# The channel mixer's first product by one level of Strassen's algorithm, its second product as a stage of its own

## The chip, the core and the metric

The kernel runs on one core of one Trainium2 chip. A core has five engines with instruction streams of their own: TensorE (PE, matrix products; PEld is its loading of weights), VectorE (DVE), ScalarE (ACT), GpSimd (POOL) and SyncE (SP), which issues DMA transfers. An engine takes its instructions in order; instructions of different engines wait for one another by semaphores. On-chip memory is SBUF (128 partitions) and PSUM (eight banks of 512 float32 per partition), in which TensorE accumulates. The metric is the device time of one execution in microseconds, by the median of several runs.

## What is computed

The reference is one layer of a hybrid model on 1024 tokens of width 1024, with 16 learned tokens ahead. Three token mixers, their gates and `w_mix_out` come first; the channel mixer `conv_ffn` is the last stage:

```python
def rms_norm(x, g):
    x32 = x.astype(jnp.float32)
    y = x32 * lax.rsqrt(jnp.mean(x32 * x32, axis=-1, keepdims=True) + EPS)
    return (y * g.astype(jnp.float32)).astype(x.dtype)
...
def conv_ffn(x, w_up, dw_w, dw_b, w_down):
    h = causal_dwconv(x @ w_up, dw_w, dw_b)
    a, b = jnp.split(h, 2, axis=-1)
    return (jax.nn.silu(a) * b) @ w_down
...
        h = h + (g1 * y_hg + g2 * y_at + g3 * y_cv) @ w_mix_out[l]
        h = h + conv_ffn(rms_norm(h, norm2_g[l]), w_ffn_up[l], ffn_dw_w[l], ffn_dw_b[l], w_ffn_down[l])
    return h[:, N_META:]
```

`w_ffn_up` is 1024 x 5632 (the halves a and b of 2816 columns each), `w_ffn_down` 2816 x 1024, `w_mix_out` 1024 x 1024. The depthwise convolution has three taps in the direction of the tokens, so the first token needs two of the learned ones ahead of it: the mixer works on 1026 tokens.

## The kernel before

All three products are made to float32 accuracy out of a faster format: every operand is split into a high part and the rest (hi on ScalarE, a rounding copy; lo on VectorE or GpSimd, a subtraction), and `mm3` makes three products for each block of 128 rows of the contraction: hi x hi, hi x lo, lo x hi.

The stages before are phase 1 (norm, projections, two of the token mixers), phase 2 (attention and the sum of the three branches into `y`), the token mix and the channel mixer.

- **Token mix** (`ysplit`, `mix`, `norm2`). `ysplit` makes hi and lo of `y` (tile `yt`) in three chunks of tokens. `mix` runs over four groups of 256 output columns; for each it loads and splits four panels of `w_mix_out` (`panel`: raw tile `wur`, split tile `wu`, the lo on GpSimd) and makes 24 products (8 k x 3) of 256 columns for each of the 8 tiles of 128 tokens, and a small product for the two learned tokens (tile number -1). VectorE adds the result (PSUM tile `one`) to the residual `h1`, ScalarE sums squares. In the fourth group each tile goes straight on to `norm2`: the reciprocal root by some eleven VectorE steps on one column, ScalarE scales two half tiles (`xs`), TensorE transposes them, VectorE multiplies by the norm's gain, ScalarE and GpSimd or VectorE split the result into `x2`.
- **Channel mixer** (`up0`, `up`, `gate`, `down`). Panel pair j (of 22) is 128 columns of a and 128 of b. For each half `up` makes 3 chunks x 8 k x 3 products of 342 columns into PSUM tile `up` (`one` in `up0`, which is used for j = 0 and 1); ScalarE and VectorE apply the taps from PSUM (`ypad`), `gate` applies silu and the product, and splits the hidden panel (`hid`). `down` multiplies pairs of hidden panels by two rows of `w_ffn_down` (tile `wd`): 8 token tiles x 2 column halves x 2 panels x 3 products of 512 columns, into PSUM tile `dn`; VectorE adds each to `h1`. So `down` of two former panels runs among the `up` products of the next two; `down` of the last panel writes the output.

The order of each engine's instructions is set by a list scheduler, which takes what is ready by the program's order and by `high_priority`; tiles share memory by pools, and a pool that is opened where another was closed makes its first writer wait for the last reader of the old one (`reuse_waits`).

## Time and profile before

| | |
|---|---|
| median of 3 runs | 2007.42 us (2006.85 to 2009.17) |
| the profiled execution | 2008.94 us, of which the profile's span is 2007.1 us |
| busy, TensorE / VectorE / ScalarE / GpSimd | 96% / 64% / 37% / 18% |
| token mix, from its first product | at 1142.34 us |
| channel mixer, from the end of the last `w_mix_out` product | from about 1245.56 us to the end |

A profile is one execution. Times are microseconds from the start of the span. A matmul's end is modelled, so that the time between two starts is the better measure of TensorE's pace; in square brackets a row of the timeline names the engine's idle time before it and the instruction that ended it. The granted clock is TensorE's, as a share of full speed: its two levels are 1.2 and 2.4 GHz, so 0.52 over a stretch means that nearly all of it ran at the lower.

### The profile page before, as it was taken

The numbers are of one execution on the slowest core, as the hardware profiler recorded it, in microseconds if no ns is written. First come the engines' busy times: TensorE is split into PE (matmuls) and PEld (weight loads), VectorE is DVE, ScalarE is ACT, GpSimd is POOL, SyncE is SP. The second block draws the span as 40 slices with busy tenths as digits, with TensorE's granted clock in tenths as the row PEclk, the third lists the DMA queues.
The fourth block names the chain that finished last, engine by engine and source line by source line (L and its number), as shares of the span: only waits on it lengthen the run. The fifth ranks groups of instructions, "written<-read, shape, count | busy, mean of one in ns | idle before, by whom it ended". The sixth has DMA issues, their size and how long they took to land.

```text
span 2007.1 us, 31950 instructions
## 1 busy us (share of the span) xinstructions
PE 1925.3 (96%) x12592; PEld 1827.0 (91%) x12592; DVE 1275.3 (64%) x2661; ACT 745.1 (37%) x1559; POOL 360.8 (18%) x380
## 2 busy tenths in 40 slices
PE   5999999999999998899999899999999999999998
PEld 5989999998999998788999799899999999999997
DVE  7577988999887953547666615654554455445545
ACT  4456888212421243535454534521222122212210
POOL 4232122443423311212342222000000000000000
PEclk8999999999999999889999999999999999999999
DMA  4233332221111227453332311210111011111102
GB/s 152 51 93 100 104 101 57 65 64 48 38 46 37 64 82 157 122 140 102 102 96 58 121 43 38 90 48 29 61 54 48 27 59 58 43 31 58 55 5 84
DMA packets 153125, 142.03 MB, mean 71 GB/s; under 512 B 7178, under 2 KB 140765, under 8 KB 152334
## 3 DMA queue, kind: packets, MB, share of 16 engines
q1 hardware_dynamic: 141822, 128.27, 22.3%
q0 software_dynamic: 11152, 11.71, 2.4%
q8 instruction: 99, 1.62, 0.3%
q14 instruction: 52, 0.43, 0.1%
HBM read 108.64 MB, written 31.31 MB: 70 GB/s over the span
## 4 chain that ended last, share of the span: by engine, by line
PE 61%; DVE 9%; DMA 4%; issue 1%; ACT 1%; POOL 1%; SPq 0%; POOLq 0%; ACTq 0%; DVEq 0%
PE up L74 23%; PE dn L74 11%; PE mm L74 9%; PE one L74 7%; DVE A L835 5%; PE gt L74 2%; PE pv L1054 2%; PE pt L1044 2%; PE S L1027 2%; DMA wgr<-in_w_in_dram 1%; DMA cv_d<-H 1%; PE at L62 1%; DVE Q L762 1%; DVE att L747 1%; PE one L89 0%
## 5 line engine op out<-in xcount | busy, mean ns | idle before, releaser
L74 PE MATMUL up<-x,wu 128*128 128x342 f32 x2880 | 477.9, 320 | 0.0
L74 PEld LDWEIGHTS up<-x,wu 128*128 128x128 f32 x2880 | 463.1, 189 | 12.6
L74 PE MATMUL gt<-xn,wg 128*128 128x342 f32 x2016 | 355.1, 326 | 13.6 <-ACT tg L910 6.5
L74 PEld LDWEIGHTS gt<-xn,wg 128*128 128x128 f32 x2016 | 321.3, 190 | 18.9 <-ACT tg L910 8.4
L74 PE MATMUL dn<-wd,hid 128*128 128x512 f32 x1008 | 257.7, 393 | 1.4 <-DVE h L1355 1.3
L1355 DVE TENSOR_TENSOR h<-dn,h 128x512 f32<-128x512 f32 x176 | 120.9, 687 | 191.9 <-PE dn L74 191.7
L74 PEld LDWEIGHTS dn<-wd,hid 128*128 128x128 f32 x1008 | 184.4, 188 | 32.1 <-DVE h L1355 2.9
L835 DVE SCALAR_TENSOR_TENSOR A<-H,cvw,A 128x256 f32<-128x256 f32 (+2 forms) x210 | 186.2, 916 | 1.8
L122 ACT ACTIVATE wu<-wur 128x512 fp32r<-128x512 f32 x104 | 65.0, 627 | 310.3 <-PE up L74 284.3
L1322 DVE SCALAR_TENSOR_TENSOR ypad<-up,fpar,ypad 128x1026 f32<-128x1026 f32 x80 | 102.5, 1281 | 64.8 <-ACT ypad L1320 64.7
L1319 POOL MEMSET ypad<- 128x2 f32 x40 | 4.0, 99 | 648.6 <-DVE ypad L1330 600.5
L123 DVE TENSOR_TENSOR wu<-wur,wu 128x512 fp32r<-128x512 f32 x88 | 60.5, 688 | 89.9 <-ACT wu L122 88.6
L74 PE MATMUL mm<-bT,wo 128*128 128x386 f32 (+2 forms) x576 | 109.1, 333 | 4.9 <-ACT bT L1124 3.4
L74 PE MATMUL mm<-xn,wm 128*128 128x256 f32 (+1 forms) x768 | 101.5, 288 | 3.5 <-DVE g L551 2.0
L513 DVE TENSOR_SCALAR_CACHE_REDUCE jd<-sc,cb 128x912 bf16<-128x912 f32 (+1 forms) x124 | 102.6, 828 | 3.2
L74 PE MATMUL mm<-xn,wc 128*128 128x260 f32 x768 | 101.3, 286 | 2.5 <-DVE Q L636 2.5
L74 PEld LDWEIGHTS mm<-bT,wo 128*128 128x128 f32 x576 | 95.2, 195 | 7.9 <-ACT bT L1124 4.2
L74 PEld LDWEIGHTS mm<-xn,wm 128*128 128x128 f32 x768 | 96.7, 191 | 4.0 <-DVE Q L636 3.9
L74 PEld LDWEIGHTS mm<-xn,wc 128*128 128x128 f32 x768 | 95.4, 189 | 3.1 <-DVE Q L636 2.8
L74 PE MATMUL one<-wu,yt 128*128 128x256 f32 x768 | 94.3, 282 | 1.8 <-ACT yt L1214 1.2
L74 PEld LDWEIGHTS one<-wu,yt 128*128 128x128 f32 x768 | 91.8, 188 | 2.3 <-ACT yt L1214 1.4
L511 ACT ACTIVATE ja<-sc,cb 128x1040 bf16<-128x1040 f32 (+2 forms) x93 | 84.5, 909 | 14.1 <-DVE cb L518 8.0
(383 smaller groups left out, 2994.9 us busy)
## 6 DMA issues: line engine op xcount, KB each, us to landing
...
```

Source lines behind the costliest of these rows:

```text
L62: self.nc.tensor.matmul(*args, **kw)
L74: self.nc.tensor.matmul(ps, x(k), y(k), start=first and i == 0 and j == 0, stop=last and i == n - 1 and j == 2)
L122: nc.scalar.activation(hl[:, 0], raw, AF.Copy)
L123: (lo or nc.vector).tensor_tensor(hl[:, 1], raw, hl[:, 0], op=OP.subtract)
L511: nc.scalar.activation(ja[:, :n], self.sc[j], AF.Sign, scale=-1.0, bias=T0[:, c], accum_out=cnt[:, c])
L513: nc.vector.tensor_scalar(jd[:, :n], self.sc[j], T0[:, c], 0.0, op0=OP.is_lt, op1=OP.add, accum_out=cnt[:, c])
L835: nc.vector.scalar_tensor_tensor(acc, h, self.cvw[:, c, k:k + 1], acc, op0=OP.mult, op1=OP.add)
L1027: nc.tensor.matmul(pS[:, :w], qs[:, h, :], kst[:, part, s], start=part == 0, stop=part == 1)
L1044: nc.tensor.transpose(pt[:kn, a, i, :], P[i][:, k0:k0 + kn], self.ident)
L1054: nc.tensor.matmul(pv[:, 0:256], vt[:kn, kt, :], pT[:kn, part, a].rearrange("p a b -> p (a b)"), start=g == 0 and a == 0 and part == 0, st ...
L1322: nc.vector.scalar_tensor_tensor(v3(o), u3, wt(2 - o), v3(o), op0=OP.mult, op1=OP.add)
L1355: nc.vector.tensor_tensor(self.h1[i][:, ns], pd, self.h1[i][:, ns], op=OP.add)
```

## The change

**The first product.** For one pair j the product is a matrix of 256 rows (128 of a, 128 of b) by 1026 tokens over 1024 of contraction. It is cut in two in the direction of the contraction (4 k each), in rows (a and b), and the tokens are cut into four pieces of 256 with the two tokens ahead of each repeated (258 columns). An item is one pair of token pieces, so that item 0 is the first half of the tokens and item 1 the second. For an item the eight block products of 128 rows x 258 columns x 512 are replaced by seven, in Winograd's form: sums of weight blocks (`up_weights`: the names a11, s2, a12, s3, s1, a22, s4) times sums of token blocks (`combine`: b11, t2, b21, t3, t1, t4, b22), in the seven `STEPS`. Accumulators `acc0`, `acc1` and `acc2` take up to three steps each; between steps ScalarE copies (`us`) and VectorE adds (`u2`, `u3` and the four pieces of `u`). The sums of weights are made on GpSimd, four per j, and all seven are split by ScalarE and VectorE (before: four panels per j). The sums of tokens are made once, on VectorE.

**The token mix** runs in two halves of the tokens, so that `w_mix_out` is read and split twice (32 panels for 16). The norm of the first half (tiles -1 to 3) and its token sums stand after the first half's products, those of tiles 4 to 7 after the second's. For j = 0 the products of item 0 are written ahead of those of item 1.

**After the products of a j** `hidden` applies taps, silu and gate from SBUF (tile `u`) and writes the hidden panel to DRAM (`hid_d`); the residual goes to DRAM as well (`h1_d`, issued by GpSimd).

**The second product** is a stage of its own behind all 22 panels: for each half of the tokens 11 groups of two hidden panels, each read back with its rows of `w_ffn_down` and split there, into eight PSUM banks that stand for the whole half; the residual is added at the end. The number and size of these products is unchanged, `w_ffn_down` is read and split twice.

The diff, without the functions' removed bodies (they are printed above):

```diff
+                                      stop=last and i == n - 1 and j == 2, skip_group_check=more)
...
+        yt = [p.tile([128, 2, 8, n], F32R, name=f"yt{i}") for i, (p, n) in enumerate(zip(pools, (514, 512)))]
...
+    def wtile(self, nk):
+        return self.wp.tile([128, 1024], F32R, name="wu", bufs=9).rearrange("p (a k c) -> p a k c", a=2, k=nk)
+    def wload(self, src, k0, nk, c0, nco):
+        t = self.wp.tile([128, 512], F32, name="wur", bufs=7).rearrange("p (k c) -> p k c", k=nk)
+        self.nc.sync.dma_start(t, src[k0 * 128:(k0 + nk) * 128, c0:c0 + nco].rearrange("(k p) c -> p k c", p=128))
+        return t
+    def split(self, t, raw, lo=None):
+        self.nc.scalar.activation(t[:, 0], raw, AF.Copy)
+        (lo or self.nc.vector).tensor_tensor(t[:, 1], raw, t[:, 0], op=OP.subtract)
...
+            self.split(t, self.wload(src, k0, nk, c0, nco), self.nc.gpsimd)
...
+    def mix(self, half, yt, mp, ha, ps):
...
+        tiles = ((0, 1, -1, 2, 3), (4, 5, 6, 7))[half]
...
         for q in range(4):
+            hl = [self.panel(a["w_mix_out"][0], 2 * h, 2, 256 * q, 256) for h in range(4)]
             ws = lambda part: (lambda k: hl[k // 2][:, part, k % 2, :])
             qs = slice(256 * q, 256 * q + 256)
+            for i in tiles:
+                src, P = (self.hh, 2) if i < 0 else (self.h1[i], 128)
...
+    def operands(self, pool, s):
+        return {n: pool.tile([128, 2, 4, 258], F32R, name=f"{n}_{s}") for n in ("b11", "t2", "b21", "t3", "t1", "t4", "b22")}
+    def norm2(self, i, mp):
...
+            for d, s, w in to:
+                nc.vector.tensor_tensor(d, s, self.n2g[:, 4 * k4:4 * k4 + 4, None].to_broadcast([128, 4, w]), op=OP.mult)
+        if i >= 0:
+            nc.gpsimd.dma_start(self.h1_d[i], src)
...
+    def raws(self, pool, s):
+        self.rw = [pool.tile([128, 4, 258], F32, name=f"rw{n}_{s}") for n in range(4)]
+    def combine(self, X):
+        r11, r12, r21, r22 = self.rw
+        op = lambda d, x, y, o: self.nc.vector.tensor_tensor(d, x, y, op=o)
+        self.split(X["b11"], r11)
+        op(r12, r22, r12, OP.subtract)
+        op(r11, r12, r11, OP.add)
+        self.split(X["t2"], r11)
+        self.split(X["b21"], r21)
+        self.split(X["t3"], r12)
+        op(r12, r22, r11, OP.subtract)
+        self.split(X["t1"], r12)
+        op(r21, r21, r11, OP.subtract)
+        self.split(X["t4"], r21)
+        self.split(X["b22"], r22)
+    def up_weights(self, j):
+        nc = self.nc
+        w = self.a["w_ffn_up"][0]
+        r21, r22, r11, r12 = (self.wload(w, 4 * h, 4, 128 * mt, 128) for h, mt in ((0, 22 + j), (1, 22 + j), (0, j), (1, j)))
+        W = {n: self.wtile(4) for n in ("a11", "s2", "a12", "s3", "s1", "a22", "s4")}
+        op = lambda d, x, y, o: nc.gpsimd.tensor_tensor(d, x, y, op=o)
+        self.split(W["a11"], r11)
+        self.split(W["a12"], r12)
+        self.split(W["a22"], r22)
+        op(r11, r11, r21, OP.subtract)
+        op(r21, r21, r22, OP.add)
+        op(r22, r22, r11, OP.subtract)
+        self.split(W["s2"], r22)
+        self.split(W["s3"], r11)
+        self.split(W["s1"], r21)
+        op(r12, r12, r22, OP.subtract)
+        self.split(W["s4"], r12)
+        return W
+    STEPS = (("a11", "b11", 0), ("s2", "t2", 1), ("a12", "b21", 0), ("s3", "t3", 1), ("s1", "t1", 2), ("a22", "t4", 1), ("s4", "b22", 2))
+    def products(self, items, fp, ps):
+        nc = self.nc
+        n = len(items)
+        acc = [ps.tile([128, 2, 512], F32, name=f"acc{b}")[:, 0:n, 0:258] for b in range(3)]
+        s, u2, u3 = (fp.tile([128, 2, 258], F32, name=b)[:, 0:n] for b in ("us", "u2", "u3"))
+        seen = set()
+        def to(ab, pos):
+            s0 = items[0][3]
+            return items[0][2].rearrange("p a (s c) n -> p a s c n", s=2)[:, ab, s0:s0 + n, pos]
+        add = lambda d, x, y: nc.vector.tensor_tensor(d, x, y, op=OP.add)
+        for step, (wn, xn, bank) in enumerate(self.STEPS):
+            for i, (W, X, _, _) in enumerate(items):
+                w, x = W[wn], X[xn]
+                self.mm3(acc[bank][:, i], tuple((lambda k, p=p: w[:, p, k, :]) for p in (0, 1)),
+                         tuple((lambda k, p=p: x[:, p, k, :]) for p in (0, 1)), list(range(4)), first=bank not in seen, more=True)
+            seen.add(bank)
+            A, B, C = acc
+            if step == 0:
+                nc.scalar.activation(s, A, AF.Copy)
+            elif step == 1:
+                add(u2, B, s)
+            elif step == 2:
+                nc.scalar.activation(to(0, 0), A, AF.Copy)
+            elif step == 3:
+                add(u3, B, s)
+            elif step == 4:
+                add(to(1, 1), C, u3)
+            elif step == 5:
+                add(to(1, 0), B, s)
+            else:
+                add(to(0, 1), C, u2)
+    def hidden(self, j, u, ys, fp):
+        nc = self.nc
+        for half, y in enumerate(ys):
+            wt = lambda k: self.fpar[:, k, 22 * half + j:22 * half + j + 1]
+            nc.scalar.activation(y, u[:, half, :, 2:258], AF.Identity, scale=wt(2), bias=wt(3))
+            for o in (1, 0):
+                nc.vector.scalar_tensor_tensor(y, u[:, half, :, o:o + 256], wt(o), y, op0=OP.mult, op1=OP.add)
+        A, B = ys
         nc.scalar.activation(A, A, AF.Silu)
         nc.vector.tensor_tensor(A, A, B, op=OP.mult)
+        nc.sync.dma_start(self.hid_d[j], A.rearrange("p c n -> p (c n)"))
+    def down(self, dp, ps):
         nc, a = self.nc, self.a
         out = self.out[0]
+        for half in range(2):
+            acc = [ps.tile([128, 512], F32, name=f"d{b}") for b in range(8)]
+            for g in range(11):
+                ks = (2 * g, 2 * g + 1)
+                hd, wd = [], []
+                with self.tc.high_priority(130):
+                    for k in ks:
+                        wr = dp.tile([128, 1024], F32, name="wdr", bufs=3)
+                        hr = dp.tile([128, 512], F32, name="hdr", bufs=3)
+                        nc.sync.dma_start(wr, a["w_ffn_down"][0][128 * k:128 * k + 128, :])
+                        nc.sync.dma_start(hr, self.hid_d[k][:, 512 * half:512 * half + 512])
+                        wd.append(dp.tile([128, 2, 1024], F32R, name="wd", bufs=6))
+                        hd.append(dp.tile([128, 2, 512], F32R, name="hd", bufs=6))
+                        self.split(wd[-1], wr)
+                        self.split(hd[-1], hr)
+                if g == 5:
+                    hf = [dp.tile([128, 1024], F32, name="hf", bufs=4) for _ in range(4)]
+                    for i in range(4):
+                        nc.sync.dma_start(hf[i], self.h1_d[4 * half + i])
+                for i in range(4):
+                    ts = slice(128 * i, 128 * i + 128)
+                    for c in range(2):
+                        ns = slice(512 * c, 512 * c + 512)
+                        self.mm3(acc[2 * i + c], tuple((lambda k, p=p: hd[k][:, p, ts]) for p in (0, 1)),
+                                 tuple((lambda k, p=p: wd[k][:, p, ns]) for p in (0, 1)), [0, 1], first=g == 0, last=g == 10)
+                        if g == 10:
+                            nc.vector.tensor_tensor(hf[i][:, ns], acc[2 * i + c], hf[i][:, ns], op=OP.add)
+                            rows = slice(512 * half + 128 * i, 512 * half + 128 * i + 128)
+                            if half and i == 3:
+                                nc.sync.dma_start(out[rows, ns], hf[i][:, ns])
+                            elif c:
+                                nc.sync.dma_start(out[rows, :], hf[i])
+    def mixer(self, yp):
...
+        self.mix(0, yt[0], mp, ha, ps)
+        off("yt1", "y")
+        X = [self.operands(on("x0", side="right"), 0)]
+        self.raws(on("rw0", side="right"), 0)
+        for i in range(-1, 4):
+            self.norm2(i, mp)
+        self.combine(X[0])
+        off("rw0", "ha")
+        self.mix(1, yt[1], mp, None, ps)
+        off("yt2")
+        with self.tc.high_priority(500):
+            W = [self.up_weights(0)]
+        X.append(self.operands(on("x1", side="right"), 1))
+        self.raws(on("rw1", side="right"), 1)
+        for i in range(4, 8):
+            self.norm2(i, mp)
+        self.combine(X[1])
+        off("rw1", "mx", "hb", "ps4")
+        ps = on("ps5", space=PSUM)
+        fp = on("ff")
+        for j in range(22):
+            ys = [fp.tile([128, 4, 256], F32, name="yc", bufs=3) for _ in range(2)]
+            u = fp.tile([128, 2, 4, 258], F32, name="u", bufs=2)
+            items = [(W[j], X[s], u, s) for s in range(2)]
+            if j == 0:
+                self.products(items[:1], fp, ps)
+                W.append(self.up_weights(1))
+                self.products(items[1:], fp, ps)
+            else:
+                self.products(items, fp, ps)
+            if j + 2 < 22:
+                W.append(self.up_weights(j + 2))
+            self.hidden(j, u, ys, fp)
+        off("ff", "x1", "x0", "wu", "ps5", "ps3")
+        dp = on("dw", side="right")
+        self.down(dp, on("ps6", space=PSUM))
+        off("dw", "ps6")
```

The scheduler places the new instructions as follows. The first place is GpSimd's order at the start of the token mix (`y` are the last sums of phase 2, `wu` the lo splits of `w_mix_out` panels, `yh` a copy for the learned tokens). Before:

```order
L1171 TENSOR_TENSOR y_1_9167<-y_1_9167,tg 128x384
L1065 COPY pT<-sm 128x512 x2
L123 TENSOR_TENSOR wu<-wur,wu 128x512
L1171 TENSOR_TENSOR y_2_9147<-y_2_9147,tg 128x256
L123 TENSOR_TENSOR wu<-wur,wu 128x512
```

and after:

```order
L1172 TENSOR_TENSOR y_2_9192<-y_2_9192,tg 128x256
L1172 TENSOR_TENSOR y_2_9195<-y_2_9195,tg 128x256
L1172 TENSOR_TENSOR y_2_9198<-y_2_9198,tg 128x256
L82 COPY yh<-yt_12531 128x8x32
L83 COPY yh<-yt_12531 128x8x2
L1229 TENSOR_TENSOR wu<-wur,wu 128x512 x21
```

Six panels were split among the last sums of phase 2; now the first split stands behind all of them and behind the copies of `yt`. The ring `wu` has grown from 6 tiles to 9 and `wur` from 2 to 7, and its memory is that of an operand of phase 2's last products: the first panel's transfer and the first copy into `yt0` wait for the last product of phase 2.

The second place is the start of the channel mixer, on TensorE (transposes are `dn<-ident,xs`). Before, from the last `w_mix_out` products:

```order
L74 MATMUL one<-wu,yt_12525 128x256 x24
L74 MATMUL one<-x_12546,wu 128x344
L1273 MATMUL dn<-ident,xs 128x128 x8
L74 MATMUL one<-x_12546,wu 128x344 x42
L1273 MATMUL dn<-ident,xs 128x128 x8
L74 MATMUL one<-x_12546,wu 128x344 x5
L1273 MATMUL dn<-ident,xs 128x128 x12
L74 MATMUL one<-x_12546,wu 128x344 x2
L1273 MATMUL dn<-ident,xs 128x128 x4
L74 MATMUL one<-x_12546,wu 128x344 x46
L1273 MATMUL dn<-ident,xs 128x128 x8
```

and after (`acc0`, `b11_0` is step 0 of item 0, and so on):

```order
L1293 MATMUL dn_14041<-ident_167,xs_14042 128x128 x4
L75 MATMUL acc0_14184<-b11_0_13232,wu_13975 128x258 x12
L75 MATMUL acc1_14185<-t2_0_13233,wu_13976 128x258 x12
L75 MATMUL acc2_14186<-t1_0_13236,wu_13979 128x258 x6
L1293 MATMUL dn_14068<-ident_167,xs_14069 128x128 x4
L75 MATMUL acc2_14186<-t1_0_13236,wu_13979 128x258 x6
L1293 MATMUL dn_14077<-ident_167,xs_14078 128x128 x4
L1293 MATMUL dn_14103<-ident_167,xs_14104 128x128 x4
L1293 MATMUL dn_14111<-ident_167,xs_14112 128x128 x4
L1293 MATMUL dn_14136<-ident_167,xs_14137 128x128 x4
L1293 MATMUL dn_14144<-ident_167,xs_14145 128x128 x4
L75 MATMUL acc0_14184<-b21_0_13234,wu_13977 128x258 x12
```

Where 96 products stood among the transposes, 36 stand now. The next one waits for item 0's first copy and add, and those stand, on ScalarE and VectorE, behind the sums of tokens of item 1; VectorE's order there is

```order
L1302 TENSOR_TENSOR rw1_1_14014<-dn_14136,par_166 128x4x128
L1302 TENSOR_TENSOR rw3_1_14016<-dn_14144,par_166 128x4x128
L1316 TENSOR_TENSOR rw1_1_14014<-rw3_1_14016,rw1_1_14014 128x1032
L1229 TENSOR_TENSOR b22_1_14009<-rw3_1_14016,b22_1_14009 128x1032
L1316 TENSOR_TENSOR rw0_1_14013<-rw1_1_14014,rw0_1_14013 128x1032
L1229 TENSOR_TENSOR t3_1_14006<-rw1_1_14014,t3_1_14006 128x1032
L1316 TENSOR_TENSOR rw2_1_14015<-rw2_1_14015,rw0_1_14013 128x1032
L1229 TENSOR_TENSOR t2_1_14004<-rw0_1_14013,t2_1_14004 128x1032
L1316 TENSOR_TENSOR rw1_1_14014<-rw3_1_14016,rw0_1_14013 128x1032
L1229 TENSOR_TENSOR t4_1_14008<-rw2_1_14015,t4_1_14008 128x1032
L1229 TENSOR_TENSOR t1_1_14007<-rw1_1_14014,t1_1_14007 128x1032
L1363 TENSOR_TENSOR u2_14188<-acc1_14185,us_14187 128x258
```

The first two rows empty the transposes of tile 7; nine steps follow, and only then `u2`.

The third place is ScalarE's order at the end of the up products. Before, `wd` was split well ahead, among the taps:

```order
L1320 ACTIVATE ypad<-up,fpar 128x1026
L1329 ACTIVATE ypad<-ypad 128x1024
L1320 ACTIVATE ypad<-up,fpar 128x1026
L122 ACTIVATE wd<-wdr 128x1024 x2
L1332 ACTIVATE hid<-ypad 128x1024
```

and after (`yc<-u,fpar x2` are the tap passes of the last j):

```order
L1376 ACTIVATE u<-acc_18943 128x2x258
L1395 ACTIVATE yc<-yc 128x1024
L1391 ACTIVATE yc<-u,fpar 128x1024 x2
L1228 ACTIVATE wd<-wdr 128x1024
L1228 ACTIVATE hd<-hdr 128x512
L1228 ACTIVATE wd<-wdr 128x1024
```

The first splits for the down stage stand behind the tap passes of the last j, which need all of its products.

## Rows read from the trace of the kernel before

**Rows 1.** The page: the span, and each engine's busy time and share.

```profile
span 2007.1 us, 31950 instructions
PE 1925.3 (96%) x12592; PEld 1827.0 (91%) x12592; DVE 1275.3 (64%) x2661; ACT 745.1 (37%) x1559; POOL 360.8 (18%) x380
```

**Rows 2.** Windows: start:end, length; busy PE, PEld, DVE, ACT, POOL; clock, DMA share, GB/s.

```profile
1245.56:1273.76 28.20, 23.25 (x141) 21.52 (x139) 19.56 (x52) 13.38 (x25) 5.90 (x5) 0.88 0.24 75
1474.00:1541.46 67.46, 67.46 (x387) 63.42 (x386) 32.68 (x39) 15.59 (x19) 0.40 (x4) 1.00 0.16 47
1255.00:1260.00 5.00, 1.32 (x9) 0.84 (x8) 4.60 (x13) 2.56 (x6) 2.31 (x2) 0.80 0.73 253
1260.00:1265.00 5.00, 4.89 (x19) 4.43 (x20) 4.37 (x12) 2.96 (x6) 0.00 (x0) 0.52 0.00 0
```

**Rows 3.** The chain that ended last: start, length, engine and group.

```profile
1138.43 2.79 DMA wur<-in_w_mix_out_dram
...
1151.18 22.72 PE one L74 x192
...
1474.00 22.72 PE up L74 x144
```

**Rows 4.** Timeline of TensorE, two stretches: start, length, instruction and count.

```profile
448.98 8.77 PE L74 MATMUL mm<-xn,wc 128*128 128x260 f32 x72
457.59 0.66 PE L62 MATMUL at<-Q,K 128*128 128x64 f32 x5
...
1496.56 2.89 PE L74 MATMUL dn<-wd,hid 128*128 128x512 f32 x12
1499.29 2.98 PE L74 MATMUL up<-x,wu 128*128 128x342 f32 x18
```

**Rows 5.** Timeline of VectorE and GpSimd in phase 1, two stretches.

```profile
471.76 1.27 POOL L123 TENSOR_TENSOR wc<-wcr,wc 128x512 fp32r<-128x512 f32 x1 [1.55 <-ACT wc L122]
...
471.85 2.27 DVE L835 SCALAR_TENSOR_TENSOR A<-H,cvw,A 128x1026 f32<-128x1026 f32 x1
...
485.52 1.28 DVE L835 SCALAR_TENSOR_TENSOR A<-H,cvw,A 128x1026 f32<-128x1026 f32 x1
485.66 2.31 POOL L765 TENSOR_TENSOR K<-K,tot 128x512 f32<-128x512 f32 x1 [5.55 <-PE at L62]
```

**Rows 6.** Timeline of TensorE at the start of the token mix.

```profile
1139.81 1.36 PE L74 MATMUL mm<-atT,bT 128*128 128x256 f32 x10
1142.34 1.62 PE L74 MATMUL one<-wu,yt 128*128 128x256 f32 x10 [1.17 <-ACT yt L1214]
1144.54 1.68 PE L74 MATMUL one<-wu,yt 128*128 128x256 f32 x12 [0.59 <-DVE yt L1215]
```

**Rows 7.** Timeline of TensorE at the start of the up products.

```profile
1245.56 0.33 PE L74 MATMUL one<-x,wu 128*128 128x344 f32 x1
...
1260.09 1.11 PE L1273 MATMUL dn<-ident,xs 128*128 128x128 f32 x4 [3.55 <-ACT xs L1270]
```

**Rows 8.** Groups of instructions after 1246: count | busy, mean ns | idle before.

```profile
L1322 DVE SCALAR_TENSOR_TENSOR ypad<-up,fpar,ypad 128x1026 f32<-128x1026 f32 x80 | 102.5, 1281 | 64.8 <-ACT ypad L1320 64.7
L123 DVE TENSOR_TENSOR wu<-wur,wu 128x512 fp32r<-128x512 f32 x85 | 58.5, 688 | 85.7 <-ACT wu L122 84.4
L122 ACT ACTIVATE wu<-wur 128x512 fp32r<-128x512 f32 x85 | 53.3, 627 | 291.0 <-PE up L74 284.3 <-PE one L74 3.4 <-DMA wur<-in_w_ffn_up_dram 2.0
L1330 DVE TENSOR_TENSOR ypad<-ypad 128x1024 f32<-128x1024 f32 x22 | 26.9, 1222 | 1.7 <-ACT ypad L1329 1.4
L1332 ACT ACTIVATE hid<-ypad 128x1024 fp32r<-128x1024 f32 x22 | 23.3, 1061 | 103.0 <-DVE ypad L1330 103.0
L122 ACT ACTIVATE wd<-wdr 128x1024 fp32r<-128x1024 f32 x22 | 22.1, 1050 | 3.7 <-PE dn L74 2.3 <-DMA wdr<-in_w_ffn_down_dram 1.4
L1270 ACT ACTIVATE xs<-h,rq_yn 128x512 f32<-128x512 f32 x8 | 5.3, 715 | 5.4 <-DVE rq_hn L99 4.2 <-DVE rq_yn L106 1.2
```

**Rows 9.** Instructions on tile `yt`: duration in ns, min/median/max.

```profile
L1214 ACT ACTIVATE yt<-y x24: 401/508/513, 1141.8 to 1150.6; 128x386 fp32r<-128x386 f32 x8, 128x384 fp32r<-128x384 f32 x8, 128x256 fp32r<-128x256 f32 x8
```

212 lines of the change are left out of this document (66 added, 146 removed).

## The prediction

> **What bounds the kernel now.** I read the page's shares first: TensorE is busy 96% of the span [rows 1]. Then one period of the channel mixer by windows: in the 67.46 us from 1474.00, TensorE is busy all 67.46, VectorE 32.68, ScalarE 15.59, GpSimd 0.40, the DMA engines 0.16 of the time, at granted clock 1.00 [rows 2]. So inside the mixer a product saved is time saved, until VectorE's load (half a period now) becomes the period. Then the edges of the stage: between the last `w_mix_out` product and the steady up products, 28.20 us hold 23.25 of TensorE, at clock 0.88 [rows 2, 7]. The change takes from the first and adds to the second, so both are priced.
>
> **The pace of products.** 144 products of 342 columns take 22.72 us, 157.8 ns each; 192 of 256 take 22.72, 118.3 ns [rows 3]. Seventy-two of 260 columns run from 448.98 to the next product at 457.59, 119.6 ns each; twelve of 512 from 1496.56 to 1499.29, 227.5 ns [rows 4]. For 258 columns I take 119.3, nearer to the closer neighbour's.
>
> **What is removed.** The mixer's first product goes from 3168 products of 342 columns (44 panels of 72) to 22 panels of 168 (7 steps, 2 items, 4 k, 3 terms), 3696 of 258. 3168 x 0.1578 = 499.9; 3696 x 0.1193 = 440.9: **-59 us**, between -58 by the 260 row and -63 by the 256 row. The second product keeps its 1056 products of 512 columns.
> The Trainium skill ("TensorE: Matmul & The Clock Gate", Part 1) gives a product N divided by 2.4 GHz plus about 2.5 ns: 110 ns for 258 columns and 145 for 342, so -53. The rows are slower at both widths and are what this kernel's operands reach, so the rows decide.
>
> **Does VectorE keep up with a panel of 168 x 0.1193 = 20.04 us?** It now has, per panel, 7 lo splits of 0.688, 5 adds of 516 columns at the same, 4 tap steps of 1.28 and the gate of 1.22 [rows 8]: 4.82 + 3.44 + 5.12 + 1.22 = 14.6. ScalarE has 7 hi splits of 0.627, two copies of 516 like them, two tap passes and a Silu of 1.06: 8.8. GpSimd gets 4 combinations of weight panels of 128x512, each 1.27 by its split [rows 5]: 5.1. They run side by side only if they don't block each other, and rows show that they do. A VectorE step that reads two SBUF tensors, begun at 471.85 under a GpSimd step (471.76, 1.27), took 2.27, where it takes 1.28 alone; the other way about, the GpSimd step of 485.66 began under such a VectorE step (485.52, 1.28) and took 2.31 [rows 5]. In the new panel 11.2 of VectorE's 14.6 us read two SBUF tensors (splits, taps, gate; the adds read one from PSUM). If every GpSimd step pushed VectorE back by its whole length it would need 14.6 + 5.1 = 19.7 us of 20.04. I take no loss in the steady panels. The accumulators: by the order of the program 33 to 38 other products (3.9 to 4.5 us) lie between a step's last product and the next use of its accumulator, against an add of 0.69 and the one or two steps queued ahead of it. The weight ring runs about a panel ahead; 1 MB of weights and 0.5 MB of `hid` a panel are 75 GB/s, against 253 shown [rows 2].
> The Trainium skill ("SBUF — State Buffer", "SBUF: two separate sides") has a rule against this change: VectorE with two SBUF inputs and a GpSimd step reading SBUF take one port pair in turn, and the loser is blocked for the whole instruction. The trace agrees (2.27 us is the rest of the other's 1.27 and a step's own time). By the rule the worst panel is those 19.7 us, which fits; rival 1 is the case in which it doesn't.
>
> **Place 1, the start of the token mix.** Before, six panels of `w_mix_out` have landed and are split before the phase's last products end at 1141.17; TensorE idles 1.17 + 0.59 us [rows 6]. Now the larger `wu` ring lies where that phase's last operand was, and the first panel's DMA and the first `yt0` copy both wait for its last product. The DMA lands 2.79 after its release [rows 3]: 1144.2 with handovers. Meanwhile ScalarE does 16 `yt0` copies of 0.51 or less [rows 9], some 6 us: 1147.3; behind them one `yt1` copy of 0.4, then `wu` hi of 0.63: 1148.5. GpSimd's lo of 1.27 holds the second term after that. So some 7.5 us idle where 1.8 were; and after a stop the rows show clock 0.52 for 5 us [rows 2]; an estimate for products at that clock is 1.5 lost. **+7** (+4, if copies pass faster, to +10).
>
> **Inside the token mix.** The first half's norm and operands are made while the second half's products run, with nothing due soon; but 32 panels' lo splits on GpSimd (32 x 1.27 = 41 us in about 100) and VectorE's two-tensor steps stand in each other's way, and a late split holds a product. **+3** (0 to +6).
>
> **Place 2, the start of the up products.** Before, 28.20 us [rows 2] hold 96 products (15.2) and 40 transposes of 0.11 (4.4): 8.6 lost, the largest part one wait of 3.55 [rows 7] and the slow clock behind it. Now only item 0's operands are there; item 1's come from tiles 4 to 7. The norms of tiles 5 to 7 (ScalarE's scaling, 0.72 a half tile [rows 8], and eleven small VectorE steps a tile) put tile 7's transposes about 15 us after the last `w_mix_out` product, 22 if GpSimd's splits push every VectorE step. Then two evictions of 0.69 and nine steps over 128x1032 at 1.22 [rows 8]: 12.4 us. Behind all of them in VectorE's order stands `u2`, item 0's first add, and `us` stands behind the hi splits on ScalarE; TensorE's third step waits for both. It has 36 products (4.3) and 32 transposes (3.5) for 28 us: 20 idle; 2 more for slow clock and 1.5 for the gaps between j = 0's steps of one item (12 products, 1.43 us, against an add of 0.43). So 23.5 against 8.6: **+15** (+9, if half of the operands' steps slip in ahead of the transposes, to +22, by the blocked chain).
>
> **Place 3, the start of the down stage.** Before there was no border: `dn` products ran among `up` ones. Now the last product's accumulator is added (0.69), two tap passes on ScalarE (1.06 each) wait for that, and the hi splits of `wd` (1.05) and `hd` (0.63) stand behind them [rows 8]: 4.5, with handovers 5. The lo of `wd` stands behind tap steps on VectorE: 0.6. Slow clock after the stop, as above, 1.5. **+7** (+5 to +9). Each later group of 48 products (10.9 us) needs 3.4 of ScalarE, 3.8 of VectorE and 1.5 MB (141 GB/s): covered, as are `hid` and `h1` on their way through DRAM, which are written long before they are read; if not, rival 3.
>
> **What else goes.** From 1245.56 to the span's end are 761.5 us [rows 1, 7] for 499.9 + 1056 x 0.2275 = 740.1 of products; 21.4 are lost, 8.6 of them at place 2, the other 12.8 in switching between `up` and `dn`, at the first `dn` groups, and behind the last product. That last part stays, some 4, and of the other 9 I take 6 as gone: **-6** (-3 to -8).
>
> **Sum.** -59 + 7 + 3 + 15 + 7 - 6 = -33. The profiled execution took 2008.94 for a span of 2007.1 [rows 1], 1.5 over the median of 2007.42: 2008.94 - 33 = 1975.9, by the median 1974.4. Between them, with the places rather short than long: 1976.
>
> **Rivals.**
> 1. VectorE sets the panel. For it: with GpSimd's 5.1 only 0.3 us are left, and the adds stand in a fixed order behind splits and taps that wait their turn [rows 5]. Against it: GpSimd also meets adds, which it doesn't hold, and 3.9 us of slack. At 0.6 us a panel 21 x 0.6 = 13: 1989. From 33 / 21 = 1.6 us a panel the gain is gone; at 2 us 1976 + 42 = 2018, slower. That is the case on the other side.
> 2. The edges cost less: places 1 and 2 at their low ends, and no loss inside the token mix, -3 - 6 - 3: 1964.
> 3. The down stage starves: 22 groups, each behind four splits on two engines that queue with DMAs on one SP queue. For it: `wd` is read twice. Against: each engine is under 40% busy there. At 0.5 us a group +11: 1987.
> That the products aren't saved can't be: their count and width stand in the program.
>
> **How the numbers follow.** Forecast 1976 (1966 to 1986): 0.65. Rival 2 (1956 to 1966): 0.12. Rival 3 (1986 to 1994): 0.08. Rival 1: 0.15, of it 0.05 up to 2003, 0.03 within 0.2% of the median, 0.07 above. 0.2%, 4 us, is about what a measurement here can tell from no change. Faster 0.65 + 0.12 + 0.08 + 0.05 = 0.90; same 0.03; slower 0.07. The range leaves out the lower half of rival 2 and most of 1: 1962 to 1994.
>
> **What would show it.** Right: panels that repeat every 20.0 to 20.2 us at clock 1.00 with 168 products and no gap, VectorE 14.6 to 18 us of each; 7 to 8 us idle before the first `one`; about 20 in 28 before step 2 of j = 0, ended by `us` or `u2`; 5 before `d0`. Wrong: panels of 20.6 us or more that wait for VectorE's adds, with two-tensor steps over 2 us in each; waits for `wd` or `hd` inside the down stage; 258 columns far from 119 ns.

## The result and the profile after

The changed kernel takes 1976.35 us, median of 4 runs (1974.80 to 1977.86), where the kernel before took 2007.94 beside it (2006.85 to 2009.17): ratio 0.984, 95% interval 0.9825 to 0.986. The forecast was 1976. The profiled execution took 1977.86 us for a span of 1976.1; the rows below are its.

The page, its span and busy times (compare [rows 1]):

```profile
span 1976.1 us, 33818 instructions
PE 1872.8 (95%) x13120; PEld 1778.5 (90%) x13120; DVE 1361.3 (69%) x2733; ACT 842.6 (43%) x1727; POOL 511.4 (26%) x440
```

TensorE works 52 us less, the span is 31 shorter: the other 21 became waits. Timeline of TensorE at the three borders (compare [rows 6] and [rows 7]), in brackets the wait and what ended it:

```profile
1139.83 2.81 PE L75 MATMUL mm<-atT,bT 128*128 128x256 f32 x22
1148.57 0.80 PE L75 MATMUL one<-wu,yt 128*128 128x256 f32 x2 [5.94 <-ACT wu L1228]
...
1255.00 1.27 PE L1293 MATMUL dn<-ident,xs 128*128 128x128 f32 x8
1258.56 1.72 PE L75 MATMUL acc<-b,wu 128*128 128x258 f32 x12 [2.28 <-DVE h L1269]
...
1270.80 1.97 PE L1293 MATMUL dn<-ident,xs 128*128 128x128 f32 x8 [4.22 <-ACT xs L1291]
1284.46 2.95 PE L75 MATMUL acc<-b,wu 128*128 128x258 f32 x12 [11.70 <-ACT us L1372]
...
1721.83 3.04 PE L75 MATMUL acc<-b,wu 128*128 128x258 f32 x24
1729.57 70.78 PE L75 MATMUL d<-wd,hd 128*128 128x512 f32 x300 [4.71 <-ACT hd L1228]
```

Windows at the same places and in the stages' middle (columns as in [rows 2]):

```profile
1142.64:1150.00 7.36, 1.43 (x5) 1.10 (x5) 7.20 (x15) 7.33 (x22) 3.03 (x5) 0.85 0.71 236
1150.00:1203.40 53.40, 53.39 (x436) 52.84 (x436) 26.32 (x64) 25.62 (x76) 27.73 (x24) 0.96 0.48 165
...
1260.00:1284.46 24.46, 7.32 (x52) 6.21 (x50) 21.31 (x40) 10.28 (x12) 2.28 (x2) 0.65 0.08 28
1284.46:1304.50 20.04, 20.04 (x154) 20.04 (x155) 8.22 (x16) 5.84 (x11) 3.58 (x3) 0.92 0.19 54
1304.50:1404.70 100.20, 100.20 (x838) 100.20 (x837) 75.82 (x85) 43.62 (x60) 31.13 (x21) 1.00 0.26 80
1729.57:1751.00 21.43, 21.43 (x83) 17.47 (x84) 17.66 (x19) 11.87 (x15) 0.00 (x0) 0.88 0.86 301
1751.00:1971.70 220.70, 220.70 (x974) 182.49 (x972) 74.08 (x87) 54.93 (x72) 0.00 (x0) 1.00 0.44 148
```

In the panels (fifth row) TensorE never stops, at granted clock 1.00; a panel of 168 products repeats every 20.13 us, 119.8 ns a product. VectorE works 15.2 us in each, GpSimd 6.3. At place 2 (third row) VectorE is busy 21.31 of 24.46 us and TensorE 7.32. Groups of the panels, 1300 to 1720 us:

```profile
L1393 DVE SCALAR_TENSOR_TENSOR yc<-u,fpar,yc 128x1024 f32<-128x1024 f32 x84 | 127.1, 1538 | 9.6 <-ACT yc L1391 9.6
L1336 POOL TENSOR_TENSOR wur<-wur 128x512 f32<-128x512 f32 x80 | 122.2, 1527 | 276.2 <-DVE wu L1229 273.0
L1229 DVE TENSOR_TENSOR wu<-wur,wu 128x512 fp32r<-128x512 f32 x141 | 103.8, 743 | 7.7 <-ACT wu L1228 7.5
L1363 DVE TENSOR_TENSOR u<-acc,us 128x516 f32<-128x516 f32 x62 | 42.7, 688 | 60.5 <-PE acc L75 57.2 <-ACT yc L1391 3.3
```

Taps take 1.54 for the 1.28 of [rows 8], GpSimd's sums 1.53 for 1.27: the two hold each other up, as in [rows 5], but VectorE still waits for TensorE before its adds (57.2 us ahead of 62 of them), not the other way.

Place 2 by VectorE and ScalarE, 1268 to 1290 us:

```profile
1271.95 0.69 DVE L1302 TENSOR_TENSOR rw<-dn,par 128x512 f32<-128x512 f32 x1 [2.04 <-PE dn L1293]
1273.53 1.23 DVE L1316 TENSOR_TENSOR rw<-rw,rw 128x1032 f32<-128x1032 f32 x1
1281.54 2.45 DVE L1229 TENSOR_TENSOR t<-rw,t 128x1032 fp32r<-128x1032 f32 x2
...
1284.02 0.39 ACT L1372 ACTIVATE us<-acc 128x258 f32<-128x258 f32 x1 [1.30 <-DVE t L1229]
```

Two evictions and nine steps of 1.23 stand ahead, as forecast. `us` begins 0.03 after the last lo split ends, with ScalarE idle before it: it reads `acc0` alone, which has long been ready, but in the program its tile takes memory that the raw token sums held, so it waits for their last reader. Place 3, 1720 to 1735 us:

```profile
1724.90 0.70 DVE L1363 TENSOR_TENSOR u<-acc,u 128x516 f32<-128x516 f32 x1 [2.18 <-PE acc L75]
1725.68 2.37 ACT L1391 ACTIVATE yc<-u,fpar 128x1024 f32<-128x1024 f32 x2 [10.74 <-DVE u L1363]
1727.96 1.04 ACT L1228 ACTIVATE wd<-wdr 128x1024 fp32r<-128x1024 f32 x1
1728.91 0.61 ACT L1228 ACTIVATE hd<-hdr 128x512 fp32r<-128x512 f32 x1
```

The last add, two tap passes, then the two hi splits: 4.7 us, in that order.

### The profile page after: what moved, and what is told of

It reads as the page before. It is cut to its first block, busy times and chain, and to the rows that moved or that the text cites. A ratio compares the mean times of both kernels' runs of the same rounds, so it can differ in the third digit from the quotient of the medians.

```text
span 1976.1 us, 33818 instructions
## 1 busy us (share of the span) xinstructions
PE 1872.8 (95%) x13120; PEld 1778.5 (90%) x13120; DVE 1361.3 (69%) x2733; ACT 842.6 (43%) x1727; POOL 511.4 (26%) x440
## 4 chain that ended last, share of the span: by engine, by line
PE 58%; DVE 11%; DMA 4%; ACT 2%; issue 1%; POOL 0%; SPq 0%; ACTq 0%; DVEq 0%; POOLq 0%
PE acc L75 22%; PE d L75 12%; PE mm L75 10%; DVE A L836 5%; PE one L75 3%; PE gt L75 2%; PE pv L1055 2%; PE pt L1045 2%; PE S L1028 2%; DMA wgr<-in_w_in_dram 1%; DMA cv_d<-H 1%; PE at L62 1%; DVE Q L763 1%; DVE att L748 1%; DVE rw L1316 1%
## 5 line engine op out<-in xcount | busy, mean ns | idle before, releaser
L75 PEld LDWEIGHTS gt<-xn,wg 128*128 128x128 f32 x2016 | 322.6, 191 | 18.4 <-ACT tg L911 9.5
L75 PE MATMUL acc<-t,wu 128*128 128x258 f32 x2112 | 264.5, 282 | 0.0
L75 PEld LDWEIGHTS acc<-t,wu 128*128 128x128 f32 x2112 | 258.1, 189 | 0.0
L75 PE MATMUL d<-wd,hd 128*128 128x512 f32 x1056 | 242.1, 392 | 4.7 <-ACT hd L1228 4.7
L75 PEld LDWEIGHTS d<-wd,hd 128*128 128x128 f32 x1056 | 200.0, 189 | 46.7 <-ACT hd L1228 4.9
L75 PE MATMUL acc<-b,wu 128*128 128x258 f32 x1584 | 202.6, 283 | 14.0 <-ACT us L1372 11.7
L1336 POOL TENSOR_TENSOR wur<-wur 128x512 f32<-128x512 f32 x88 | 134.6, 1530 | 311.8 <-DVE wu L1229 307.6
L75 PEld LDWEIGHTS acc<-b,wu 128*128 128x128 f32 x1584 | 195.8, 190 | 14.6 <-ACT us L1372 12.1
L1393 DVE SCALAR_TENSOR_TENSOR yc<-u,fpar,yc 128x1024 f32<-128x1024 f32 x88 | 132.1, 1527 | 11.0 <-ACT yc L1391 11.0
L1229 DVE TENSOR_TENSOR wd<-wdr,wd 128x1024 fp32r<-128x1024 f32 x44 | 53.8, 1222 | 124.2 <-ACT wd L1228 124.2
L1229 DVE TENSOR_TENSOR wu<-wur,wu 128x512 fp32r<-128x512 f32 x154 | 115.1, 754 | 13.0 <-ACT wu L1228 12.8
```

Source lines behind the costliest of these rows:

```text
L75: self.nc.tensor.matmul(ps, x(k), y(k), start=first and i == 0 and j == 0, stop=last and i == n - 1 and j == 2, skip_group_check=more)
L1229: (lo or self.nc.vector).tensor_tensor(t[:, 1], raw, t[:, 0], op=OP.subtract)
L1336: op = lambda d, x, y, o: nc.gpsimd.tensor_tensor(d, x, y, op=o)
L1393: nc.vector.scalar_tensor_tensor(y, u[:, half, :, o:o + 256], wt(o), y, op0=OP.mult, op1=OP.add)
```

## The experiments

All runs are the changed kernel with an edit, but for one (e9), which is the changed kernel again. The kernel before took 2014 to 2019 us on the chips of these runs, so times are compared by their ratio to it; the changed kernel, run again on one of them, had 0.983 (0.9813 to 0.9847). The stages ahead of the token mix, which no edit touches, end anywhere from 1142.6 to 1150.5 us, so an edge is read from the traces from there on. Worked out from the timelines' rows of TensorE (last `mm`, last `one`, last `acc`, first and last `d`), in us:

| run | token mix | up stage | idle before down | down stage | from the last `mm` to the end |
|---|---|---|---|---|---|
| changed kernel | 112.4 | 469.8 | 4.71 | 242.1 | 833.5 |
| changed kernel again (e9) | 111.9 | 471.7 | 4.71 | 242.5 | 835.2 |
| eight products (e1) | 112.3 | 514.3 | 3.59 | 242.5 | 876.9 |
| sums on VectorE (e2) | 112.4 | 470.8 | 4.71 | 241.6 | 833.8 |
| more GpSimd, 8 (e3) | 111.8 | 524.6 | 4.71 | 241.7 | 887.1 |
| more GpSimd, 4 (e5) | 112.5 | 497.3 | 4.71 | 242.1 | 861.3 |
| mix start (e4; again, e11) | 109.3; 109.4 | 471.5; 469.7 | 4.71; 4.71 | 242.4; 242.0 | 832.3; 830.1 |
| down early (e6) | 112.4 | 469.7 | none | 240.0 | 826.3 |
| item 0 first (e7) | 112.8 | 463.3 | 4.71 | 241.6 | 826.7 |
| the same, sums on VectorE (e12) | 112.4 | 462.1 | 4.71 | 241.8 | 825.3 |
| all edges (e8; again, e10) | 109.5; 109.5 | 458.7; 458.7 | none | 239.9; 239.9 | 812.6; 812.7 |

**What the seven products are worth.** The stages, pools and widths stay, but each output is the plain sum of two block products, with no sums of tokens or weights.

```diff
-    STEPS = (("a11", "b11", 0), ("s2", "t2", 1), ("a12", "b21", 0), ("s3", "t3", 1), ("s1", "t1", 2), ("a22", "t4", 1), ("s4", "b22", 2))
+    OUTS = ((0, 0, 0), (0, 1, 1), (1, 0, 2), (1, 1, 0))
...
+        for ab, pos, bank in self.OUTS:
+            acc = ps.tile([128, 2, 512], F32, name=f"acc{bank}")[:, 0:n, 0:258]
+            for h in range(2):
...
+                    w, x = W[f"a{ab + 1}{h + 1}"], X[f"b{h + 1}{pos + 1}"]
```

> The stages stay as in the changed kernel (two halves of the token mix, second product on its own), but the first product is made of eight direct block products: four weight blocks and four token blocks are split, no sums are made. Theory: 22 x 24 more products of 258 columns at 0.1198 us are +63 us; against that item 1's operands need 4 steps on VectorE in the place of 11, and nothing of item 0 waits for them, which gives back most of the 20 us idle at the start of the up products: -18 to -26. Sum +37 to +45, so 2013 to 2021: Strassen's part is worth some 40 us, and the rest of the change by itself costs 5 to 13 us against the kernel before. Rival (the gain comes from the stages and not from the saved products): not above 1985.

Measured: ratio 1.0045 (1.003 to 1.006), so some 43 us over the changed kernel and 9 over the kernel before; the rival, that the stages bring the gain, is out. Its start of up, by TensorE's timeline:

```profile
1275.41 1.27 PE L1293 MATMUL dn<-ident,xs 128*128 128x128 f32 x8 [1.37 <-ACT xs L1291]
1277.20 67.96 PE L75 MATMUL acc<-b,wu 128*128 128x258 f32 x562 [0.53 <-ACT u L1345]
1780.63 19.65 PE L75 MATMUL d<-wd,hd 128*128 128x512 f32 x73 [3.59 <-ACT hd L1228]
```

Its products start 120.3 ns apart in the steady panels, not 119.8 (see the next run). So 4224 of them are 508.1 of its 514.3 us: 6 lost. The changed kernel has 3696, 442.8, and loses 27. So the sums win 65 us of products and cost 21 at place 2, while the rest of the change without Strassen (the borders of its stages, and 4224 products of 258 columns that take 8 us more than 3168 of 342) costs 9.

**Does GpSimd's part matter?** The weight sums on VectorE:

```diff
-        op = lambda d, x, y, o: nc.gpsimd.tensor_tensor(d, x, y, op=o)
+        op = lambda d, x, y, o: nc.vector.tensor_tensor(d, x, y, op=o)
```

> The four sums of weight blocks of a panel are made by VectorE in the place of GpSimd, so that GpSimd is idle in the panels. Theory (TensorE sets the panel, VectorE and GpSimd block one another but fit in): VectorE has 14.6 + 4 x 0.69 = 17.4 us of 20.1, the panel stays at 20.1 us and the time within 3 us of 1976; the mean tap step falls from 1.53 to 1.28 us and the mean lo split from 0.75 to 0.69. Rival (the shared turn with GpSimd holds the panels back): the panel falls under 20.0 us and the time by 5 us or more.

Measured: 0.9828 (0.9811 to 0.9844), no change. The groups of the panels, 1300 to 1720 us:

```profile
L1393 DVE SCALAR_TENSOR_TENSOR yc<-u,fpar,yc 128x1024 f32<-128x1024 f32 x84 | 105.7, 1280 | 1.7 <-ACT yc L1391 1.6
L1229 DVE TENSOR_TENSOR wu<-wur,wu 128x512 fp32r<-128x512 f32 x144 | 99.3, 690 | 44.3 <-ACT wu L1228 44.3
L1336 DVE TENSOR_TENSOR wur<-wur 128x512 f32<-128x512 f32 x80 | 55.2, 691 | 2.0
```

Without GpSimd beside them the taps are back at 1.28; a sum takes VectorE 0.69 where it took GpSimd 1.53. The mutual hold-up is real, and neither way sets the panel. A panel is 20.21 us here for 20.13, without a gap and at granted clock 1.00: a product takes 120.3 ns in place of 119.8, as in each run that leaves GpSimd idle in the panels (e1, e8, e10 and e12 too). Why is open.

**How much GpSimd would it take?** Eight more additions of GpSimd for each of 20 panels, into a scratch tile that nothing uses:

```diff
             W.append(self.up_weights(j + 2))
+            for _ in range(8):
+                self.nc.gpsimd.tensor_tensor(more, fill, fill, op=OP.add)
```

> Eight more GpSimd additions of 128x512 stand behind the weight sums of each of 20 panels, on a scratch tile that nothing else reads. If a two-tensor VectorE step and a GpSimd step exclude one another, GpSimd's 12 x 1.27 = 15.3 us and VectorE's 11.2 us must go one after the other: 26.5 us against 20.1 of products, panels of 25 to 27 us, 2075 to 2120 in all. If they only slow each other a little, GpSimd's 15.3 us fit into 20.1 and the time stays within 5 us of 1976.

Measured: 1.0095 (1.0075 to 1.0115): 53 us over the changed kernel, about half of the least that exclusion was to cost. Then four in place of eight:

> As the run with eight further GpSimd additions per panel, but with four (128x512, both inputs in SBUF, written to scratch; they compute nothing that is used). With eight the panel went from 20.13 to 23.1 us, and VectorE was busy some 20.3 us of it. Theory that VectorE's busy time sets where the panel breaks: its busy time per panel was 16.0 us beside 4 GpSimd steps and 20.3 beside 12, so about 18 beside 8, still under 20.1; the panel stays within 0.4 us of 20.13 and the time within 8 us of the changed kernel (ratio to the kernel before 0.984 to 0.988). Rival, each GpSimd step beyond the four costs its share of the panel at once (3.0 us for eight, so 1.5 for four): panel 21.6, time 25 to 30 us over the changed kernel (ratio 0.997 to 0.999).

Measured: 0.9956 (0.9942 to 0.997), 25 us over; the up stage is 27 us longer for 80 additions and 54 for 160, 0.34 us for each. That fits the rival's number, but the windows of this run show a reason that neither theory had:

```profile
1440.00:1480.00 40.00, 34.62 (x274) 34.21 (x274) 33.74 (x31) 15.33 (x22) 31.62 (x21) 0.96 0.25 80
1480.00:1520.00 40.00, 40.00 (x336) 40.00 (x335) 30.31 (x35) 17.34 (x25) 12.41 (x9) 1.00 0.26 80
```

The additions wait for nothing, so GpSimd ran ahead through them: up to 1467 us it is busy nearly all the time, and after that the panels are the old ones. So both runs measure one thing, the panel beside a GpSimd that never rests: with eight, 13 panels from 1325.3 to 1635.2 us, 23.84 us each. TensorE's waits for VectorE (1300 to 1720 us), two groups of VectorE in the 13 panels, and one moment (timeline of all engines, 1414 to 1424 us):

```profile
PE acc L75 <- DVE u L1363: 31.5, 14, 3.1
...
L1363 DVE TENSOR_TENSOR u<-acc,us 128x516 f32<-128x516 f32 x39 | 26.8, 687 | 17.0 <-PE acc L75 16.8 <-ACT yc L1391 0.2
L1396 DVE TENSOR_TENSOR yc<-yc 128x1024 f32<-128x1024 f32 x13 | 26.7, 2056 | 0.0
...
1419.79 4.92 POOL L1491 TENSOR_TENSOR more<-fill 128x512 f32<-128x512 f32 x3
1420.31 2.06 DVE L1396 TENSOR_TENSOR yc<-yc 128x1024 f32<-128x1024 f32 x1
1422.29 0.68 DVE L1363 TENSOR_TENSOR u<-acc,us 128x516 f32<-128x516 f32 x1
1422.90 0.92 DVE L1229 TENSOR_TENSOR wu<-wur,wu 128x512 fp32r<-128x512 f32 x1
```

TensorE waits for VectorE's adds, as rival 1 said it would: in the 13 panels it stands still for 34.5 us, 2.7 a panel (28.4 for those adds, 5.9 for a copy of ScalarE's), and the other 1.1 of 3.7 go with a slower clock, 0.97 on average. VectorE's gate takes 2.06 for its 1.21 in all 13 and the add from PSUM its usual 0.69; in the moment shown GpSimd's three additions, 1.04 each alone, take 4.92, which is 1.80 more, about VectorE's 1.21 + 0.69 of work on two SBUF tensors. This is the alternation that the Trainium skill describes ("SBUF — State Buffer", "SBUF: two separate sides"), and here the trace agrees with it. Over a whole panel it can't be complete: 11.2 us of such VectorE work and 14.5 GpSimd steps (4 x 1.28 + 10.5 x 1.04, by 52 sums and 137 additions in the 13 panels) make 27.2, more than 23.84. Successive steps overlap a little (VectorE's of 1.23 start 1.14 apart), which by estimate accounts for some 2 us; the rest stays open.

**Place 1.** The raw weight ring lower in memory, the first four panels ahead of `ysplit`, and the loads of the residual behind them:

```diff
+            raw = self.wload(src, k0, nk, c0, nco)
+            t = self.wtile(nk)
+            self.split(t, raw, self.nc.gpsimd)
...
+        self.first = [self.panel(self.a["w_mix_out"][0], 2 * h, 2, 0, 256) for h in range(4)]
+        with self.tc.issue_after(self.made):
+            yt = self.ysplit((y1, y2))
```

> Only the start of the token mix: the raw ring of weight panels lies where memory is free before phase 2 ends, the residual's loads are queued behind the first panels, and ScalarE's hi splits of the first four panels stand ahead of the yt copies. Theory (the 7.4 us idle is a path of its own, DMA, copies, hi split): about 2 us idle, so -5 to -7 with the slow clock behind it: 1969 to 1971. Rival (GpSimd's lo splits or the norm of the first half are next and just as late): 0 to -2, with new waits inside the token mix.

> The edge of the token mix alone once more (the raw weight ring placed so that four panels of w_mix_out are loaded and split ahead of the split of y), beside the changed kernel on the same chip. Its trace had 2.8 us of idle TensorE there for 5.9 and the same slow clock behind it: 2 to 4 us less than the changed kernel. Rival, the ratio of its first timing was the chip's and the edge gives nothing: within 1.5 us.

Measured: 0.9827 (0.9807 to 0.9847) and 0.9825 (0.9807 to 0.9843), beside the changed kernel's 0.983: by times, not to be told apart. By the traces the stage is 2.5 to 3.1 us shorter both times. Timelines of ScalarE and TensorE, first run (its last `mm` ends at 1147.53):

```profile
1147.56 1.67 ACT L1228 ACTIVATE wu<-wur 128x512 fp32r<-128x512 f32 x3 [13.35 <-PE mm L75]
1149.14 4.22 ACT L1214 ACTIVATE yt<-y 128x386 fp32r<-128x386 f32 x12
...
1149.70 1.77 PE L75 MATMUL one<-wu,yt 128*128 128x256 f32 x10 [2.17 <-ACT yt L1214]
1152.07 6.63 PE L75 MATMUL one<-wu,yt 128*128 128x256 f32 x38 [0.60 <-DVE yt L1215]
```

The weights were what the first product waited for; now it is `yt`, 2.8 us for 5.9. My 5 to 7 was too much: the raw panels land earlier, but their hi splits still begin only with the last `mm`, and the first copy of `yt` stands behind three of them, 1.6 us after it, where the changed kernel's first copy (1142.67) begins 0.04 after.

**Place 3.** The first down group's loads and splits ahead of the last panel's taps and gate:

```diff
-            self.hidden(j, u, ys, fp)
...
+            if j < 21:
+                self.hidden(j, u, ys, fp)
...
+        ready = self.group(dp, 0, 0)
+        with self.tc.issue_after(self.made):
+            self.hidden(21, u, ys, fp)
```

> One edit of the changed kernel: the first group of the down stage has its loads and splits of w_down and hid ahead of the last panel's taps and gate, which are queued behind them on ScalarE. Theory of the prediction's place 3 (the stop is the splits' place in two queues): the 4.7 us of idle TensorE ahead of the first down product fall to under 1 us, and the slow clock behind them (2.5 us) goes with them: 5 to 7 us less than the changed kernel, ratio to the kernel before 0.981 to 0.982. Rival: the last panel's hidden values are needed soon, or the accumulators of the up stage lie in banks that the first down products need, and the stop moves behind the first products: 0 to 2 us less (0.983 to 0.984).

Measured: 0.9789 (0.9769 to 0.9809). TensorE's timeline:

```profile
1726.86 3.04 PE L75 MATMUL acc<-b,wu 128*128 128x258 f32 x24
1729.74 70.65 PE L75 MATMUL d<-wd,hd 128*128 128x512 f32 x309
```

and the window behind its first `d`:

```profile
1729.74:1751.20 21.46, 21.39 (x95) 17.35 (x94) 19.49 (x21) 13.48 (x17) 0.00 (x0) 1.00 0.96 355
```

The stop is gone, and the down stage, the same 1056 products, is 2 us shorter, which was the slow clock behind the stop: 95 products at granted clock 1.00 where 83 stood at 0.88. Together 7.

**Place 2.** All seven steps of item 0 of j = 0 ahead of item 1's token sums, with `us` of j = 0 and item 0's `u2` and `u3` in memory of their own, and item 1 begun with the two steps that need no sums; the ring of raw weight tiles is cut from seven to six:

```diff
+        zp = on("z")
...
+        self.run(self.products([(W[0], X[0], u, 0)], None, ps, zp))
+        self.plain(X[1])
+        rest = self.products([(W[0], X[1], u, 1)], None, ps, zp, (0, 2, 1, 3, 4, 5, 6))
+        next(rest)
+        with self.tc.issue_after(self.kept):
+            self.combine(X[1])
```

> One edit of the changed kernel at place 2: for the first panel pair all seven steps of the first half of the tokens are queued ahead of the second half's token sums, with their copies and additions, and the second half begins with the two steps that need no sums. Theory of place 2 (the third step waits for an accumulator's copy and addition that stand behind token sums in two queues): the wait of 11.7 us falls to about 7, since the last tile's normalised values and its nine token sums are still to be waited for; 3 to 5 us less than the changed kernel (ratio to the kernel before 0.982 to 0.983). Rival, the wait is the tokens' alone (tiles 5 to 7 come late whatever the order): within 1.5 us of the changed kernel (0.984).

Measured: 0.9775 (0.9756 to 0.9795). TensorE's timeline:

```profile
1276.44 1.41 PE L1293 MATMUL dn<-ident,xs 128*128 128x128 f32 x8 [1.87 <-ACT xs L1291]
1277.50 6.05 PE L75 MATMUL acc<-b,wu 128*128 128x258 f32 x36
1284.29 0.38 PE L75 MATMUL acc<-t,wu 128*128 128x258 f32 x1 [0.74 <-ACT t L1228]
1285.51 3.14 PE L75 MATMUL acc<-b,wu 128*128 128x258 f32 x24 [0.84 <-ACT u L1386]
```

No wait there is over 2.2 us any more, all of them together are 10.0 us for 19.4, and the up stage is 7 us shorter, more than expected: item 0's 48 further products, 5.7 us, and two of item 1's steps stand where the 11.7 were. So most of the wait was order and shared memory (changed together here, and the ring with them), not the tokens.

**All three together**, with the weight sums on VectorE (all of them, not a share):

> The three edges together: the raw weight ring placed so that the token mix's first panels are loaded and split ahead of the split of y (as in the earlier run, 3 us), the first down group ahead of the last panel, the first half's seven steps ahead of the second half's sums, and the weight sums' and token sums' work shared between VectorE and GpSimd at the start of up. Theory that the edges are independent: their gains add, 3 + 6 + 4 and a little for the sharing, 11 to 15 us less than the changed kernel, 1962 to 1966 for the kernel before at 2008 (ratio 0.977 to 0.979). Rival, that a gain at one edge is given back at the next by the slower clock or the same queue: 4 to 8 us less (0.980 to 0.982).

> The changed kernel itself once more, on one chip with the run that follows, since the ratios of the single edits stand to the kernel before as it ran beside them. Every theory expects the ratio of its first timing, 0.984, within 0.002, and a place 2, place 3 and panel that read as in its first profile.

> The three edges together once more, beside the changed kernel on the same chip. Theory that the edges' gains add: 11 to 16 us less than the changed kernel. Rival, given back at the next edge: 4 to 8 us less.

Measured: 1961.61, 0.9719 (0.9698 to 0.9739); again beside the changed kernel's 1980.08: 1959.38, 0.9722 (0.9707 to 0.9738). That is 21 us less than the changed kernel and 57 less than the kernel before on that chip, the fastest of all. The edges add, and give some 4 more than their sum: 3 + 7 + 7 are 17, 812.6 against 833.5 and 835.2 are 21 and 23, where I expected 11 to 16. One last run asked whether the weight sums' engine is what the rest comes from, with e7's edit and e2's together:

> The run with the first half's steps ahead of the second half's token sums, and the sums of weights on VectorE as well. With all edges together the up stage (last w_mix_out product to last product of the first product) took 458.7 us, with the first half's order alone 463.3, with the changed kernel 469.8 to 471.7, and with the weight sums on VectorE alone 470.8. Theory that GpSimd's steps in the start of up held VectorE back once the order no longer hid it: 459 to 460 us. Rival, that the token mix's ring edge frees the last norms earlier: it stays at 462 to 464 us.

Measured: 0.9802 (0.9789 to 0.9816); up stage 462.1. GpSimd was not it, or for 1 us net: by the product that begins the seventh panel the stage is 2.4 us ahead of e7's, and the later panels, at 120.3 ns a product, give half of it back. The number is the rival's, but its mechanism isn't there: VectorE empties the last tile's transposes 15.8 us after the last `one` in this run and with all edges. What differs is VectorE's order behind that, here and then with all edges (timelines of 1271 to 1292 us):

```profile
1286.28 1.89 DVE L1229 TENSOR_TENSOR wu<-wur,wu 128x512 fp32r<-128x512 f32 x3
1288.09 1.23 DVE L1229 TENSOR_TENSOR t<-rw,t 128x1032 fp32r<-128x1032 f32 x1
...
1286.08 1.22 DVE L1229 TENSOR_TENSOR t<-rw,t 128x1032 fp32r<-128x1032 f32 x1
1288.77 1.88 DVE L1229 TENSOR_TENSOR wu<-wur,wu 128x512 fp32r<-128x512 f32 x3
```

In e12 item 1's last token sum comes later in that order, and its split behind three splits of the next panel's weights; TensorE waits 2.40 and 2.08 us for the two. With all edges the split stands ahead of the three, and neither wait is there. By j = 0's last product that is 4.6 us, of which 3.4 stay. So the other 3.4 us of the up stage are again a place in a queue; which edit made the scheduler choose that order wasn't separated.

## Why the prediction was right

- **Up products, -59.** 3696 x 119.8 ns are 442.8 for 499.9: -57. The pace was 119.8, the 260-column row's 119.6 rather than the 119.3 taken. By the rule of the Trainium skill ("TensorE: Matmul & The Clock Gate", Part 1) it would have been 110 ns, an estimate from its formula; the trace doesn't agree.
- **VectorE keeps up.** 20.13 us a panel against 20.04, no gap, VectorE 15.2 us (14.6 to 18 forecast). Rival 1's mechanism is there (taps of 1.54), but its price isn't: a GpSimd that never rests costs 3.7 us a panel. At 0.34 us for each further step, its point of 1.6 us a panel would be some nine GpSimd steps a panel in place of four, an estimate from those two runs that holds only if the cost grows evenly from four steps on, which neither shows.
- **Place 1, +7, and the token mix, +3.** From the last `mm` to the last `one` 112.4 us for 104.4: +8.0. The wait is 5.94 for 7.5 forecast, in place of 1.8, mostly since the 17 copies ahead of the first weight split took 5.3 us and not 6.5; the slow clock behind it lasts longer than taken (5 products in 1.43 us, and 436 products in 53.39 that at the 118.3 ns of [rows 3] are 51.6): 2.6 for 1.5. So place 1 is +7 by two errors that cancel, and for the mix's inside +1 is left: no product waits for a split there. That step, +3, was the one mis-sized.
- **Place 2, +15.** From 1255.00 to 1284.46 are 29.46 us with 36 products and 32 transposes, 7.8: 21.7 lost. The next 20.04 us hold 154 products, 18.4: 1.6 more. 23.3 for the 23.5 forecast, against 8.6: +14.7. The chain was the one forecast, up to its last link: `us` did not stand in a queue but waited for memory.
- **Place 3, +7.** 4.7 idle; then 83 products in 21.43 us, which at the steady 226.6 ns (974 in 220.70) are 18.8: 2.6. Together 7.3, and e6 gives 7 back.
- **The rest, -6.** The down stage never waits (rival 3 fell). The span is 31.0 shorter; with -57.1, +8.0, +14.7, +7.3 and +1.5 in the untouched stages ahead, the rest is -5.4.

The sum missed by 2 us of 33 in the span, and no term by more than 2. That 1976 met the median of 1976.35 is partly luck: by the median the sum gave 1974.4, and the 1.6 put on top of it happened to be what it lacked. All three borders cost about what was forecast from their queues, though at place 2 the last link was memory, and e4, e6 and e7 took 3, 7 and 7 of their 30 us back, each by moving what was named or, at place 2, that and the memory.
